# Eight shifted homes for the stationary tiles of the second feed-forward product

## The chip, the core and the metric

One core of a Trainium2 chip runs one program. The metric is the device time of one execution in microseconds (us), the median of several runs. The engines are named as in the profile: PE is the matrix unit (TensorE), PEld its loads of stationary operands, DVE is VectorE, ACT is ScalarE, POOL is GpSimd, SP is the engine whose queue starts the transfers.

## What is computed

The reference is one residual block of an encoder: 256 frames of width 2048 go through a norm, a retention branch and a latent-attention branch that gates merge, and then through a feed-forward part. The change lies in the feed-forward part, which is:

```python
z = _rmsnorm(h, norm_mlp_g[l]) @ w_up[l]            # 256 x 2048  times 2048 x 8192
h = h + jnp.square(jax.nn.relu(z)) @ w_down[l]      # 256 x 8192  times 8192 x 2048
return _rmsnorm(h, norm_f_g)
```

The second product, with `w_down`, is the last large piece of work in the program; the final norm follows it.

## The kernel before

**Products in three parts.** The kernel multiplies float32 numbers with the matrix unit's fp32r type. Each operand is split into a part `hi`, its value rounded to fp32r by a copy on ACT, and a part `lo`, the remainder that DVE computes by subtracting (`split`, lines 214 to 222, for activations; `weights`, lines 146 to 153, for weights). A product is then hi times hi, hi times lo and lo times hi, three matmuls into one accumulator.

**The first feed-forward product** (lines 792 to 800) takes 64 units of 128 hidden rows. A unit (`t_unit`, lines 170 to 175) loads two pieces of `w_up` of 512 KB, splits them, and runs 16 matmuls of 512 columns (line 159) and 16 of 256 columns (line 163). There the weights are the stationary operand, the activations `hT` the moving one. ACT and DVE join the two halves of the result, apply the squared ReLU and leave the unit in `hid` in SBUF (line 800). `hid` has 64 units in all, in four tiles, one of which (`hid3`) lies in the pool `hp`.

**The second product** (lines 818 to 832) runs over the same 64 units as its contraction. For unit `i`, line 822 splits `hid` into `dh` (ACT, line 216) and `dl` (DVE, line 217), each 128 partitions by 256 frames. Line 825 loads, casts and subtracts two halves of `w_down[i]`, each 128 by 1024. `down` (lines 807 to 816) then issues three matmuls for each of 2 frame blocks `t` and 4 column blocks `c`. In all three the stationary operand is a 128 by 128 block of `dh` (lines 814 and 815) or `dl` (line 816), and the moving operand is 512 columns of the weights' `hi` or `lo`. So a unit has 24 matmuls, each with a stationary load of its own, and the whole product has 1536. The results stay in eight PSUM accumulators `pd` over all 64 units. The last two units (`LAST`) are kept back and issued column block by column block, so that the accumulators end one after another and `finish` and `normalize` can begin.

**Where the tiles lie.** A tile is taken from a pool under a tag. Tiles of one tag share `bufs` homes (fixed addresses) in rotation, and a tile's first writer waits until the readers of the tile that had the home before are done. `dh` and `dl` have 3 homes each, of 256 float32, which is 1024 bytes in every partition. The weights' `hi` and `lo` have 4 homes each of 4096 bytes (line 143). In the program before, every home that the second product's matmuls read, stationary or moving, begins at byte 128 modulo 512 of its partition, and the blocks within it (128 frames, 512 columns) are whole multiples of 512 bytes. The same holds for nearly all other products of the kernel. One stage differs: the latent projection at `w_ckv` has weight tiles of 2 rows of 288 columns (1152 bytes), so that its moving operand begins at 128 for one row and at 256 modulo 512 for the other, while its stationary operand `x` is at 128.

**What sets the order.** A scheduler orders each engine's instructions by simulating the program; an engine then runs its own list in order. Matmuls of the last two units are held in the written order. All weight loads are issued from SP's queue into 5 homes `raw`.

Of the kernel before, what the change touches and what calls it, by code (L numbers as in the profile page):

```python
# [13 lines left out]
F32R = mybir.dt.float32r  # L14
# [5 lines left out]
P = 128  # L20
S = 256
# [10 lines left out]
QK_SCALE = float(192.0 ** -0.5)  # L32
LOWEST = -3.4e38
WARM = 8
MASKED = -3.0e38

MAGIC = 12582912.0
# [15 lines left out]
def _consts():  # L53
    c = np.zeros((P, N_CONST), np.float32)
    c[:, C_ID : C_ID + P] = np.eye(P)
    p = np.arange(P)
    own = np.where(p[None, :] // CHUNK <= p[:, None] // CHUNK, 0.0, MASKED)
    c[:, C_MASK : C_MASK + 128] = own
# [30 lines left out]
def block_kernel(ctx: ExitStack, tc: tile.TileContext, A):  # L89
# [46 lines left out]
    def atps(name):  # L136
        return pat.tile([P, 512], F32, tag="at", name=name)
# [8 lines left out]
    def weights(src, shape):  # L146
        raw, hi, lo = (wtile(kind, shape) for kind in ("raw", "hi", "lo"))
        load = nc.sync.dma_start(raw, src)
        if uid[0] < 40:
            tc.keep_in_program_order(load)  # L150
        SC.copy(hi, raw)  # L151
        V.tensor_tensor(out=lo, in0=raw, in1=hi.bitcast(F32), op=ALU.subtract)  # L152
        return hi, lo
# [60 lines left out]
    def split(hi, lo, val, scale=None):  # L214
        if scale is None:
            SC.copy(hi, val)  # L216
            V.tensor_tensor(out=lo, in0=val, in1=hi.bitcast(F32), op=ALU.subtract)
        else:
            SC.activation(hi, val, AF.Copy, scale=scale)
            V.scalar_tensor_tensor(  # L220
                lo, in0=val, scalar=scale, in1=hi.bitcast(F32), op0=ALU.mult, op1=ALU.subtract
            )
# [12 lines left out]
    spin = atps("spin")  # L235
    for _ in range(WARM):
        PE.matmul(spin, cold[:, :P], cold, start=True, stop=True)
# [529 lines left out]
    hp = ctx.enter_context(tc.tile_pool(name="hp", bufs=1))  # L767
# [39 lines left out]
    def down(i, t, c, w, hs):  # L807
        (hi, lo), (dh, dl) = w, hs
        ts = slice(t * P, (t + 1) * P)
        ws = slice(c % 2 * 512, c % 2 * 512 + 512)  # L810
        out = pd[t][c]
        end = i == FT - 1
        mm = tc.keep_in_program_order if i >= FT - LAST else (lambda ins: ins)
        mm(PE.matmul(out, dh[:, ts], hi[:, ws], start=i == 0, stop=False))  # L814
        mm(PE.matmul(out, dh[:, ts], lo[:, ws], start=False, stop=False))  # L815
        mm(PE.matmul(out, dl[:, ts], hi[:, ws], start=False, stop=end))  # L816

    tail = []
    for i in range(FT):
        dh = hp.tile([P, S], F32R, tag="dh", bufs=3, name=f"dh{i}")  # L820
        dl = hp.tile([P, S], F32R, tag="dl", bufs=3, name=f"dl{i}")
        split(dh, dl, hid[i // KT][:, i % KT])
        ws = []
        for half in range(2):
            w = weights(A["w_down"][i][:, half * 1024 : (half + 1) * 1024], [P, 1024])
            ws.append(w)
            if i < FT - LAST:
                for t in range(2):
                    for c in (2 * half, 2 * half + 1):
                        down(i, t, c, w, (dh, dl))  # L830
        if i >= FT - LAST:
            tail.append((i, ws, (dh, dl)))
# [113 lines left out]
```

## Time and profile before

| | |
|---|---|
| Median of 3 runs | 1631.72 us (1631.48 to 1631.87) |
| The profiled execution | 1632.22 us, of which its span is 1630.4 us |
| First product, by its chain of work | from about 925 to 1272.7 us of the span |
| Second product: first matmul to the start of the last | 1272.7 to 1620.6 us of the span |
| PE busy over the span | 1614.9 us (99%) |
| DVE busy, ACT busy | 996.2 us (61%), 809.7 us (50%) |
| Granted matrix clock over the span | 0.998 of full speed |
| HBM read | 300.84 MB, 186 GB/s over the span |

Times are from the span's start. The busy time of a matmul in the profile runs from its start to its modelled end, and overlaps that of the next one. How long a matmul holds the engine up is therefore read from the starts of two neighbours (the *step*), not from its own duration: in the second product a matmul lasts 389 ns, but the next begins well before that.

### The profile page before, as it was taken

To read this page: it belongs to the slowest core of one execution; us is meant where nothing else is said; L and a number is where in the kernel's file an instruction comes from. 1 tells how busy PE (TensorE), PEld (TensorE's weight loads), DVE (VectorE), ACT (ScalarE), POOL (GpSimd) and SP (SyncE) were. 2 spreads that over 40 slices of the span, in tenths; PEclk is the share of its full clock that TensorE was granted. 3 is DMA by queue.
4 is the path that set the end of the run, shared out by engine and by line. 5 is a ranking of instruction groups with operands and counts; after the bars stand their busy time and mean duration, and the time that the engine had idled before them with its cause. 6 is when DMAs were issued, how large, how long until landed. Compare 5 with 4: busy or idle time off the path is not lost.

```text
span 1630.4 us, 23041 instructions
## 1 busy us (share of the span) xinstructions
PE 1614.9 (99%) x8782; PEld 1398.8 (86%) x8782; DVE 996.2 (61%) x1491; ACT 809.7 (50%) x1249; POOL 49.5 (3%) x62
## 2 busy tenths in 40 slices
PE   8999999999999999999999999999999999999997
PEld 6888888888889889888888888888888888888886
DVE  7974588655556658666765555555555555555555
ACT  6544555544445556765545544444444444444444
POOL 7100000000000000000000000000000000000001
PEclk9999999999999999999999999999999999999999
DMA  8665544555556554325575555555555655555553
GB/s 306 200 233 193 187 156 166 169 192 186 190 170 203 190 191 146 125 94 176 186 246 187 174 193 188 192 189 186 191 192 184 223 194 192 193 193 195 192 194 112
DMA packets 84480, 304.46 MB, mean 187 GB/s; under 512 B 9360, under 2 KB 9488, under 8 KB 83600
## 3 DMA queue, kind: packets, MB, share of 16 engines
q1 hardware_dynamic: 84368, 302.98, 55.3%
q8 instruction: 69, 1.13, 0.3%
q14 instruction: 43, 0.35, 0.1%
HBM read 300.84 MB, written 2.10 MB: 186 GB/s over the span
## 4 chain that ended last, share of the span: by engine, by line
PE 97%; DVE 1%; issue 0%; DMA 0%; ACT 0%; POOL 0%; SPq 0%; DVEq 0%; POOLq 0%; ACTq 0%
PE z L159 14%; PE z L163 8%; PE dn L816 7%; PE dn L814 7%; PE dn L815 7%; PE rg L159 4%; PE yr L159 4%; PE gr L159 4%; PE gm L159 4%; PE mo L159 4%; PE qk L159 2%; PE gr L163 2%; PE yr L163 2%; PE gm L163 2%; PE rg L163 2%; PE mo L163 2%
## 5 line engine op out<-in xcount | busy, mean ns | idle before, releaser
L152 DVE TENSOR_TENSOR lo<-raw,hi 128x1024 fp32r<-128x1024 f32 (+2 forms) x562 | 666.0, 1204 | 521.6 <-ACT hi L151 248.3
L151 ACT CAST hi<-raw 128x1024 fp32r<-128x1024 f32 (+2 forms) x562 | 580.8, 1035 | 536.9 <-PE z L159 135.2
L159 PE MATMUL z<-hT,hi 128*128 128x512 f32 x1024 | 245.5, 391 | 0.0
L159 PEld LDWEIGHTS z<-hT,hi 128*128 128x128 f32 x1024 | 188.0, 188 | 36.1
L815 PE MATMUL dn<-lo,dh 128*128 128x512 f32 x512 | 199.2, 389 | 0.0
L816 PE MATMUL dn<-hi,dl 128*128 128x512 f32 x512 | 199.2, 389 | 0.0
L814 PE MATMUL dn<-hi,dh 128*128 128x512 f32 x512 | 198.9, 389 | 0.0
L163 PEld LDWEIGHTS z<-hT,lo 128*128 128x128 f32 x1024 | 131.6, 191 | 5.1
L163 PE MATMUL z<-hT,lo 128*128 128x256 f32 x1024 | 133.1, 283 | 0.0
L815 PEld LDWEIGHTS dn<-lo,dh 128*128 128x128 f32 x512 | 96.1, 188 | 20.1
L816 PEld LDWEIGHTS dn<-hi,dl 128*128 128x128 f32 x512 | 96.1, 188 | 19.9
L814 PEld LDWEIGHTS dn<-hi,dh 128*128 128x128 f32 x512 | 96.1, 188 | 19.8
L216 ACT CAST dh<-hid 128x256 fp32r<-128x256 f32 x64 | 26.0, 407 | 89.3 <-PE dn L815 89.3
L159 PE MATMUL mo<-my,hi 128*128 128x512 f32 x256 | 65.5, 396 | 0.4 <-DVE val L207 0.4
L159 PE MATMUL rg<-x,hi 128*128 128x512 f32 x256 | 64.0, 395 | 0.0
L159 PE MATMUL yr<-ry,hi 128*128 128x512 f32 x256 | 61.4, 391 | 0.0
L159 PE MATMUL gr<-x,hi 128*128 128x512 f32 x256 | 61.3, 391 | 0.0
L159 PE MATMUL gm<-x,hi 128*128 128x512 f32 x256 | 61.1, 391 | 0.0
L159 PEld LDWEIGHTS gm<-x,hi 128*128 128x128 f32 x256 | 47.0, 188 | 9.1
L159 PEld LDWEIGHTS gr<-x,hi 128*128 128x128 f32 x256 | 47.0, 188 | 9.0
L159 PEld LDWEIGHTS yr<-ry,hi 128*128 128x128 f32 x256 | 46.9, 188 | 9.0
L159 PEld LDWEIGHTS rg<-x,hi 128*128 128x128 f32 x256 | 46.2, 188 | 8.6
(271 smaller groups left out, 2239.1 us busy)
## 6 DMA issues: line engine op xcount, KB each, us to landing
raw<-w_up SPq DMA_DIRECT2D x128, 512.0 KB, 4.2
raw<-w_down SPq DMA_DIRECT2D x128, 512.0 KB, 4.3
raw<-w_rv SPq DMA_DIRECT2D x32, 512.0 KB, 4.5
raw<-w_rg SPq DMA_DIRECT2D x32, 512.0 KB, 4.5
raw<-w_gret SPq DMA_DIRECT2D x32, 512.0 KB, 4.3
raw<-w_ret_o SPq DMA_DIRECT2D x32, 512.0 KB, 4.6
raw<-w_gmla SPq DMA_DIRECT2D x32, 512.0 KB, 4.4
raw<-w_out SPq DMA_DIRECT2D x32, 512.0 KB, 3.7
```

The costliest lines, as they stand in the source:

```text
L151: SC.copy(hi, raw)
L152: V.tensor_tensor(out=lo, in0=raw, in1=hi.bitcast(F32), op=ALU.subtract)
L159: PE.matmul(out, w[0][:, k], x.both(k0 + k), start=start and k == 0, stop=False)
L163: PE.matmul(out[:, :S], w[1][:, k], x.hi(k0 + k), start=False, stop=stop and k == n - 1)
L216: SC.copy(hi, val)
L814: mm(PE.matmul(out, dh[:, ts], hi[:, ws], start=i == 0, stop=False))
L815: mm(PE.matmul(out, dh[:, ts], lo[:, ws], start=False, stop=False))
L816: mm(PE.matmul(out, dl[:, ts], hi[:, ws], start=False, stop=end))
```

## The change

The tiles `dh` and `dl` get eight tags each in place of one tag with 3 homes, chosen by the unit's number modulo 8, with one home for each tag. Each tile is allocated with 16 more float32 in every partition, of which none is used: only the first 256 columns are handed on. Nothing else is edited.

```diff
 WARM = 8
+SHIFT, SHIFTS = 16, 8
 MASKED = -3.0e38
...
     for i in range(FT):
-        dh = hp.tile([P, S], F32R, tag="dh", bufs=3, name=f"dh{i}")
-        dl = hp.tile([P, S], F32R, tag="dl", bufs=3, name=f"dl{i}")
+        dh, dl = (
+            hp.tile([P, S + SHIFT], F32R, tag=f"{kind}{i % SHIFTS}", name=f"{kind}{i}")[:, :S] for kind in ("dh", "dl")
+        )
         split(dh, dl, hid[i // KT][:, i % KT])
```

A home is now 1088 bytes, that is twice 512 and 64 more. The homes are taken in the order `dh0`, `dl0`, `dh1`, `dl1` and so on, so each begins 64 bytes further on, modulo 512, than the one before it. The eight homes of `dh` lie at four places modulo 512 that are 128 apart, each place twice, and those of `dl` at the four places between them; together they go through all eight multiples of 64. The two frame blocks of a tile, 512 bytes apart, have the same place. The moving operands stay where they were modulo 512. The homes of both kinds take 17,408 bytes of a partition in place of 6,144.

## The prediction

> **What bounds the kernel now.** I read the page's busy shares first, then the chain of waits, then the chain in order of time for the two feed-forward products, and last the instructions in order of time.
>
> ```profile
> span 1630.4 us, 23041 instructions
> PE 1614.9 (99%) x8782; PEld 1398.8 (86%) x8782; DVE 996.2 (61%) x1491; ACT 809.7 (50%) x1249; POOL 49.5 (3%) x62
> PEclk9999999999999999999999999999999999999999
> PE 97%; DVE 1%; issue 0%; DMA 0%; ACT 0%; POOL 0%; SPq 0%; DVEq 0%; POOLq 0%; ACTq 0%
> ```
>
> The first and second line give span and busy time, the third the granted clock in 40 slices, the fourth the chain's shares. PE is the chain, at full clock. Time can only come from fewer matmuls, which the change doesn't give, or from a shorter *step*, the time from one matmul's start to the next one's.
>
> The instructions that touch the product's accumulators `dn` (count, then minimum, median and maximum duration in ns, then first and last start):
>
> ```profile
> L814 PE MATMUL dn<-hi,dh x512: 389/389/396, 1272.7 to 1620.2; 128*128 128x512 f32 x171
> L816 PE MATMUL dn<-hi,dl x512: 388/389/389, 1273.1 to 1620.6; 128*128 128x512 f32 x171
> ```
>
> From the first L814 at 1272.7 to the last L816 at 1620.6 lie 347.9 us and 1535 steps: 226.6 ns each. This holds from end to end, so no wait on a transfer, on ACT or on DVE is left in the product. Its time is 1536 steps, and nothing else.
>
> What a step is made of, I read from the first product's matmuls of half the width, in the chain in order of time (start, duration, count):
>
> ```profile
> 1249.96 0.60 PE z L163 x5
> ```
>
> Five steps of 256 columns take 0.60 us, 120 ns each. The 256 columns that a 512-column matmul has more cost 226.6 - 120.0 = 106.6 ns, 0.4164 ns a column. So 512 columns stream in 213.2 ns and 256 in 106.6 ns, and 13.4 ns of each step are **excess** over streaming. Every one of these matmuls has a stationary load (188 ns long in the page's rows) beside it.
>
> **The change part by part.** *Removed and added instructions:* none. There are 64 casts to `dh`, 64 subtractions to `dl`, 1536 loads and 1536 matmuls before and after, and no transfer is added or moved: 0 us.
>
> *More homes, 8 in place of 3.* The split of a unit may run eight units ahead. Now it waits for its home:
>
> ```profile
> 1403.22 0.41 ACT L216 CAST dh<-hid 128x256 fp32r<-128x256 f32 x1 [1.44 <-PE dn L815]
> 1403.66 0.43 DVE L217 TENSOR_TENSOR dl<-hid,dh 128x256 fp32r<-128x256 f32 x1 [0.62 <-ACT dh L216]
> ```
>
> ACT waits 1.44 us for PE and then casts for 0.41 us; DVE follows with 0.43 us. With eight homes the cast waits for the same place in PE's order, once a unit, only for a later unit's tile; behind it on ACT stand the same casts of weights. Before the product begins, five more casts and subtractions (5 x 0.41 and 5 x 0.43 us) can move up into the first product. There a unit takes 5.56 us (16 steps in 3.65 us and 16 in 1.91 in the chain in order of time), and ACT works 0.37 + 1.05 + 1.05 = 2.47 us of it, DVE 2 x 1.18 + 0.42 + 0.42 = 3.20 us. The gaps of 3.1 and 2.4 us hide them, and the casts of weights that could queue behind them themselves wait for PE to release a home. I cost this at 0; without the cover it is 0.84 us, once or twice. The waits removed from ACT gain nothing, since PE waits for none of them. The cast's own speed at a shifted address can't matter either: 0.41 us in 5.44 us.
>
> *Other addresses.* This is all that can reach PE. Now each stationary block begins at the same place modulo 512 as the moving operand. After the change that holds for 2 of the 8 homes of `dh` and none of `dl`; with two of three loads from `dh`, 1/6 of the loads keep it and 5/6 lose it. The trace of before has one long stage where operands stand apart: the latent projection with rows of 288 columns, whose second row lies 128 bytes further modulo 512.
>
> ```profile
> 514.75 0.29 PE L199 MATMUL kv<-hi,x 128*128 128x288 f32 x1
> 514.88 0.29 PE L200 MATMUL kv<-hi,x 128*128 128x288 f32 x1
> 515.01 0.29 PE L199 MATMUL kv<-hi,x 128*128 128x288 f32 x1
> 515.14 0.30 PE L200 MATMUL kv<-hi,x 128*128 128x288 f32 x1
> 515.27 0.42 PE L202 MATMUL kv<-lo,x 128*128 128x288 f32 x2
> 515.53 0.29 PE L199 MATMUL kv<-hi,x 128*128 128x288 f32 x1
> ```
>
> These are starts and durations; the fifth row is two matmuls. Six steps take 515.53 - 514.75 = 0.78 us, 130.0 ns each. By the rule from 256 and 512 columns, 288 columns should take 288 x 0.4164 + 13.4 = 133.3 ns. So the only stage whose operands stand apart in half of its matmuls has 10.0 ns of excess, 3.3 ns less. I take that as the estimate for the new homes: 1536 x 3.3 = **5.1 us** less. If the whole effect belongs to the half that stands apart, it is 6.7 ns there, and in the second product 1536 x 5/6 x 6.7 = 8.6 us. I take the smaller value, because only one distance of eight is seen, and because width and address can't be told apart in that stage.
>
> The far ends. Below: all excess goes, 1536 x 13.4 = 20.6 us; I know no row that reaches it, and half of it, 10 us, is the practical end. Above: the step isn't fixed even now. The product's first matmuls, behind the narrow ones, start at
>
> ```profile
> 1272.66 0.40 PE L814 MATMUL dn<-hi,dh 128*128 128x512 f32 x1
> ...
> 1274.05 0.39 PE L814 MATMUL dn<-hi,dh 128*128 128x512 f32 x1
> ```
>
> six steps apart (two rounds of L814, L815, L816): 1.39 us, 232 ns each, 5 ns more than the settled step with the same tiles. If loads and streams out of step cost that always, 1536 x 5/6 x 5 = 6.4 us more; if in every matmul, 7.7 us.
>
> The Trainium skill's page "TensorE: Matmul & The Clock Gate" (Step-by-step, the step on LDWEIGHTS) says that the two operands have independent read ports and that loading the next stationary tile takes no read bandwidth from the running matmul. By that rule addresses don't matter and the sum is 0. The 0.78 us above doesn't contradict it outright, but nothing in it explains 10.0 ns where 13.4 were due.
>
> **The sum** is made against the profiled execution, 1632.22 us: a span of 1630.4 and 1.8 us around it. 0 + 0 - 5.1 gives 1627.1; that execution was 0.5 us above the median of 1631.72, so the forecast for the median is **1626.6 us**.
>
> **The rivals.** *No change.* The excess belongs to the handover from one stationary tile to the next and not to addresses. For it: a 256-column and a 512-column step have the same excess, and in the settled product neither ACT's nor DVE's traffic, at half of the time, disturbs the step. Against it: the 10.0 ns of the projection. Time 1631.7 us. That is also how the rule of the Trainium skill's page would come out.
>
> *Slower.* Equal places modulo 512 are the good case: load and stream run in a settled rhythm that the 226.6 ns are the mark of. With homes that move by 64 bytes the rhythm is broken, every unit runs as the first six steps do, and PE gives back 5 ns in 5/6 of the steps: 1631.7 + 6.4 = 1638.1 us. It decides as soon as the mean step is above 226.6 + 2.1 ns, which is 0.2%. For it: those 1.39 us. Against it: they end after a few steps and follow a change of width, and the projection, whose distance changes from row to row, shows no such loss.
>
> *The large gain.* Equal places are the worst of all, and all other distances lose at least half of the excess: 1536 x 5/6 x 6.7 = 8.6 us and up to 13 us, 1623 to 1618 us. For it: all other stages, with equal places, have the same 13.4 ns. Against it: the projection's rows at distance 128 would have to be the whole of its gain.
>
> *The change doesn't do what it says:* with a scheduler between, homes could come in another order. Then the places modulo 512 still differ, as the home is 1088 bytes; I give it nothing of its own.
>
> **How the numbers follow.** Forecast, a gain of 3.3 to 7 us: 0.38. Large gain: 0.10. No change: 0.27. Slower: 0.25. Faster by over 0.2% (3.3 us, about what a measurement of this kernel can tell from no change) is 0.48, within it 0.27, slower 0.25. The forecast's own range is 1624 to 1629 us. The range that holds 8 in 10 must take in the half of the excess below, 1617, and the slower case with every step disturbed, 1639.5: **1617 to 1640 us**.
>
> **What would show it.** Right: the `dn` matmuls' first and last start lie 342 to 344 us apart in place of 347.9, and the step differs from unit to unit in a cycle of four or eight units, since a home keeps its place. Starts in three successive units that differ by nothing would show the no-change case, and a uniform 5.44 us a unit with a changed time elsewhere would show that the order of the work moved. The product's stretch should be all of the difference: the first product, up to about 1272.7 us, should not move by more than 1 us. Wrong: units above 5.44 us, or any idle time of PE behind `dh` or `dl`, which would make the zero for the extra homes false.

## The result: 7 us slower, all of it in the second product's steps

The changed kernel takes 1638.7 us (1638.22 to 1639.03) against 1631.48 us (1631.10 to 1631.87) of the kernel before: a ratio of 1.0044, 95% interval 1.0029 to 1.0059. The forecast was 1626.6 us with a range of 1617 to 1640 us; the rival called *Slower* had given 1638.1 us.

The profile after, first lines of the page, then two rows of the instructions that touch `dn` (first and last start in us), then the chain in order of time at the end of the first product (start, duration, count). The line numbers are 1 higher than before.

```profile
span 1636.5 us, 23035 instructions
PE 1623.7 (99%) x8782; PEld 1399.6 (86%) x8782; DVE 996.2 (61%) x1491; ACT 809.2 (49%) x1249; POOL 49.8 (3%) x62
```

```profile
L815 PE MATMUL dn<-hi,dh x512: 387/389/404, 1271.7 to 1626.5; 128*128 128x512 f32 x171
...
L817 PE MATMUL dn<-hi,dl x512: 387/397/400, 1272.1 to 1627.0; 128*128 128x512 f32 x171
```

```profile
1266.25 3.65 PE z L160 x16
1269.90 1.91 PE z L164 x16
```

The counts of matmuls are the same, and the first product's units are what they were, 16 steps in 3.65 us and 16 in 1.91. The second product runs from 1271.7 to 1627.0 us: 355.3 us in place of 347.9, 7.4 us more in 1535 steps, 231.5 ns a step in place of 226.7. That it began 1 us earlier says nothing of the change: with the work ahead of it the same, it begins at 1271.5 us in the second experiment below and at 1272.7 us in the kernel before.

How the units lie within it is read from ACT's casts to `dh`, one a unit, each released by PE's last reading of an earlier unit's `dh`:

```profile
1404.98 0.41 ACT L217 CAST dh<-hid 128x256 fp32r<-128x256 f32 x1 [1.51 <-PE dn L816]
...
1410.51 0.41 ACT L217 CAST dh<-hid 128x256 fp32r<-128x256 f32 x1 [1.49 <-PE dn L816]
...
1416.09 0.41 ACT L217 CAST dh<-hid 128x256 fp32r<-128x256 f32 x1 [1.51 <-PE dn L816]
```

By these rows a unit takes 5.53 and 5.58 us in turns (5.54 and 5.58 us by the starts of the matmuls), in place of 5.44 us each time. The cycle has two units, not four or eight: a home of `dh` and the one two units later, 256 bytes further on, behave alike. ACT still waits for PE; the profile shows no idle time of PE within the product.

### The profile page after: what moved, and what is told of

The parts are those of the page before. It is cut to its first block, busy times and chain, and to the rows that moved or that the text cites. A ratio compares the mean times of both kernels' runs of the same rounds, so it can differ in the third digit from the quotient of the medians.

```text
span 1636.5 us, 23035 instructions
## 1 busy us (share of the span) xinstructions
PE 1623.7 (99%) x8782; PEld 1399.6 (86%) x8782; DVE 996.2 (61%) x1491; ACT 809.2 (49%) x1249; POOL 49.8 (3%) x62
## 4 chain that ended last, share of the span: by engine, by line
PE 97%; DVE 1%; ACT 0%; DMA 0%; issue 0%; POOL 0%; SPq 0%; DVEq 0%; POOLq 0%; ACTq 0%
PE z L160 14%; PE z L164 7%; PE dn L817 7%; PE dn L816 7%; PE dn L815 7%; PE rg L160 4%; PE yr L160 4%; PE gr L160 4%; PE gm L160 4%; PE mo L160 4%; PE qk L160 2%; PE gr L164 2%; PE yr L164 2%; PE gm L164 2%; PE rg L164 2%; PE mo L164 2%
## 5 line engine op out<-in xcount | busy, mean ns | idle before, releaser
L218 DVE TENSOR_TENSOR dl<-hid,dh 128x256 fp32r<-128x256 f32 x64 | 27.2, 425 | 44.8 <-ACT dh L217 44.8
```

## The experiments

All are edits of the kernel before, except the one that says otherwise. Where `dh` and `dl` are moved, they rotate through 3 homes as before, and the place of a tile is set by a slice of a wider home, the same for eight units in a row:

```diff
+        dh = hp.tile([P, S + 128], F32R, tag="dh", bufs=3, name=f"dh{i}")[:, at_h : at_h + S]
+        dl = hp.tile([P, S + 128], F32R, tag="dl", bufs=3, name=f"dl{i}")[:, at_l : at_l + S]
```

The second to the ninth experiment have one run each. What they show is read from blocks of units within one trace, and not from their times.

Below, the *distance* is the byte where the stationary block begins minus the byte where the moving operand begins, modulo 512.

**Eight homes without a shift.**

```diff
+            hp.tile([P, S], F32R, tag=f"{kind}{i % 8}", name=f"{kind}{i}") for kind in ("dh", "dl")
```

> Eight homes each for dh and dl, but of 1024 bytes, so that every home begins at 128 modulo 512 as before. If the number of homes and the order that the scheduler makes of them cost the 7 us, a unit of 24 matmuls takes 5.53 to 5.58 us as in the changed kernel and the time is about 1638.7 us. If the addresses modulo 512 alone cost it, a unit takes 5.44 us and the time is that of before, 1631.5 us.

Measured: 1631.15 us, ratio 0.9998 (0.9989 to 1.0008), every unit 5.44 us. The number of homes and the order of the work cost nothing. What is left is the addresses, or the padding as such; the eleventh experiment separates these two.

**`dh` and `dl` moved together.** `at_h = at_l = 16 * (i // 8)` float32.

> Three homes as before, and dh and dl both begin 64 * (i // 8) bytes further on modulo 512, so that eight units in a row keep one distance to the moving operand, and no step between dh and dl. Theory of the distance (what counts is how far the stationary block stands from the moving operand modulo 256 or 512): the blocks of units at 0 and 256 take 5.44 us a unit, those at the odd multiples of 64 and at 128 and 384 take 5.5 to 5.6 us. Theory of the jump (what counts is that one load's place differs from the load before it, as dh and dl do): every block takes 5.44 us, but for single steps where a block begins.

Measured: 1636.63 us. The casts at the borders of blocks of eight units (distance 64, 128, 192, 256):

```profile
1315.01 0.41 ACT L216 CAST dh<-hid 128x256 fp32r<-128x256 f32 x1 [1.44 <-PE dn L815]
...
1359.80 0.41 ACT L216 CAST dh<-hid 128x256 fp32r<-128x256 f32 x1 [1.52 <-PE dn L815]
...
1404.41 0.41 ACT L216 CAST dh<-hid 128x256 fp32r<-128x256 f32 x1 [1.50 <-PE dn L815]
...
1448.37 0.41 ACT L216 CAST dh<-hid 128x256 fp32r<-128x256 f32 x1 [1.47 <-PE dn L815]
...
1491.91 0.41 ACT L216 CAST dh<-hid 128x256 fp32r<-128x256 f32 x1 [1.44 <-PE dn L815]
```

Eight units take 44.79, 44.61, 43.96 and 43.54 us, which is 5.60, 5.58, 5.49 and 5.44 us a unit. The blocks at 320, 384 and 448 repeat those at 64, 128 and 192. So the distance counts, with a period of 256 bytes, and no jump between `dh` and `dl` is needed for the loss: the theory of the jump falls.

**`dl` alone.** `at_h = 0`, `at_l = 16 * (i // 8)`.

> Three homes as before; dh stays at the moving operand's place, dl begins 64 * (i // 8) bytes further on modulo 512. Theory of the jump: units whose dl stands apart take 5.5 us or more, with the most at 64 and 320, and those at 0 take 5.44 us. Theory of the distance: one of three loads stands apart, so a third of what the second experiment shows for the same distance, on the step during which dl is loaded. If distance modulo 256 is what counts, the unit at 256 takes 5.44 us under both.

Measured: 1637.04 us. Casts at the borders of the blocks with `dl` at 64 (the first two) and at 256:

```profile
1315.85 0.41 ACT L216 CAST dh<-hid 128x256 fp32r<-128x256 f32 x1 [1.44 <-PE dn L815]
...
1360.21 0.41 ACT L216 CAST dh<-hid 128x256 fp32r<-128x256 f32 x1 [1.49 <-PE dn L815]
...
1448.98 0.41 ACT L216 CAST dh<-hid 128x256 fp32r<-128x256 f32 x1 [1.49 <-PE dn L815]
...
1492.50 0.41 ACT L216 CAST dh<-hid 128x256 fp32r<-128x256 f32 x1 [1.45 <-PE dn L815]
```

44.36 and 43.52 us for eight units: 5.55 us a unit at 64, as at all the other distances, and 5.44 us at 256, as at 0. This is a miss for the theory of the distance in its simple form: with one load of three apart, a third of 0.16, 0.14 and 0.05 us was due, and 0.11 us came each time. A mixture of distances costs more than its share, so the price isn't a fixed sum for each load.

**All operands moved together.** The weights' `hi` and `lo` of `w_down` get wider homes as well, and the same `at`.

> dh, dl and the weights' hi and lo all begin 64 * (i // 8) bytes further on modulo 512, so that all stay at equal places while the place moves. If a place as such is dear (a home off a multiple of 128 or 256), blocks take 5.5 us and more as in the second experiment at the same shift. If only the distance between stationary and moving operand counts, or the jump between loads, every block takes 5.44 us and the time is about 1631.5 us.

Measured: 1631.74 us, 5.44 us a unit at every place, with some 0.04 us once at each border of blocks. So none of the eight places costs anything as such.

**The moving operand alone.** `dh` and `dl` stay, `hi` and `lo` begin `16 * (i // 8)` float32 further on.

> dh and dl stay where they are; the weights' hi and lo begin 64 * (i // 8) bytes further on modulo 512. Theory of the signed distance modulo 256 (stationary minus moving): the order of the second experiment's blocks is mirrored, 5.44 us a unit at shifts 0 and 256, 5.49 us at 64 and 320, 5.57 us at 128 and 384, 5.60 us at 192 and 448. If only the size of the distance or the stationary tile's own place counts: 5.60, 5.57 and 5.49 us at 64, 128 and 192, or 5.44 us everywhere.

Measured: 1637.40 us. Borders of the blocks with the moving operand 64, 128 and 192 bytes on:

```profile
1315.81 0.41 ACT L218 CAST dh<-hid 128x256 fp32r<-128x256 f32 x1 [1.44 <-PE dn L817]
...
1359.77 0.41 ACT L218 CAST dh<-hid 128x256 fp32r<-128x256 f32 x1 [1.47 <-PE dn L817]
...
1404.40 0.41 ACT L218 CAST dh<-hid 128x256 fp32r<-128x256 f32 x1 [1.51 <-PE dn L817]
...
1449.20 0.41 ACT L218 CAST dh<-hid 128x256 fp32r<-128x256 f32 x1 [1.52 <-PE dn L817]
```

43.96, 44.63 and 44.80 us for eight units, 5.49, 5.58 and 5.60 us: the order of the second experiment mirrored. What counts is the signed distance.

**The projection with 288 columns.** Its weight tiles get rows of 2048 bytes, so that both rows keep one place, which moves by 64 bytes with each fourth of the contraction.

```diff
+            wtile("raw", shape), *(wtile(kind, [P, 2, 512])[:, :, at : at + 288] for kind in ("hi", "lo"))
...
-                w = weights(A["w_ckv"][k // 2, half], [P, 2, 288])
+                w = weights(A["w_ckv"][k // 2, half], [P, 2, 288], 16 * (k // 4))
```

> The weight tiles of the latent projection with 288 columns get rows of 2048 bytes in place of 1152, so that both rows of a tile begin at the same place modulo 512; that place moves by 64 bytes with every fourth of the contraction (moving operand 0, 64, 128, 192 bytes on). If the shorter excess of that stage (10.0 ns a step) came from its rows that stand apart, as the prediction took it, the first fourth has steps of 133.3 ns and a later one fewer. If it came from the width of 288 columns, the first fourth has 130 ns or less, and by the distances of the second product the other fourths have more: about 2, 5 and 7 ns at distances of 192, 128 and 64.

Measured: 1632.59 us. Two pairs of starts six steps apart, the first with all operands at equal places, the second at distance 128:

```profile
495.77 0.29 PE L201 MATMUL kv<-hi,x 128*128 128x288 f32 x1
...
496.56 0.29 PE L201 MATMUL kw<-hi,x 128*128 128x288 f32 x1
...
511.73 0.29 PE L201 MATMUL kv<-hi,x 128*128 128x288 f32 x1
...
512.53 0.29 PE L201 MATMUL kv<-hi,x 128*128 128x288 f32 x1
```

0.79 and 0.80 us. Over the steady steps of a fourth, the steps are 131.7 ns at distances 0 and 192 and 133.3 ns at 128 and 64. Neither expectation is met in full. Equal places give 131.7, not 133.3, so half of the 3.3 ns was there without any distance: at this width the rule from 256 and 512 columns comes out too long. And a constant 128 gives 133.3, more than equal places, although the layout of before, with 0 and 128 in turns, has 130.0. The sequence is better than either of the distances that it is made of. (The rows' pitch went from 1152 to 2048 bytes with this edit; no run separates its part.)

**Finer distances.** `at_h = at_l` = 2, 4, 8, 12, 24, 40, 56 and 60 float32, that is 8 to 240 bytes.

> dh and dl both begin 8, 16, 32, 48, 96, 160, 224 and 240 bytes beyond the moving operand's place, eight units each. If places count in lines of 64 bytes, 8 to 48 bytes take 5.44 us a unit, 96 takes 5.60, 160 takes 5.57, 224 and 240 take 5.49 us. If the distance acts in finer steps, the units lie between their neighbours: 5.46 to 5.56 us from 8 to 48 bytes, 5.45 to 5.47 us at 224 and 240. If equal places are not the best but only the best of the multiples of 64, one of these is below 5.44 us.

Measured: 1640.49 us. Borders of the blocks with 96, 160, 224 and 240 bytes (of the last block, five units):

```profile
1451.00 0.41 ACT L216 CAST dh<-hid 128x256 fp32r<-128x256 f32 x1 [1.52 <-PE dn L815]
...
1495.98 0.41 ACT L216 CAST dh<-hid 128x256 fp32r<-128x256 f32 x1 [1.52 <-PE dn L815]
...
1540.78 0.41 ACT L216 CAST dh<-hid 128x256 fp32r<-128x256 f32 x1 [1.52 <-PE dn L815]
...
1585.58 0.41 ACT L216 CAST dh<-hid 128x256 fp32r<-128x256 f32 x1 [1.52 <-PE dn L815]
...
1612.78 0.41 ACT L216 CAST dh<-hid 128x256 fp32r<-128x256 f32 x1 [1.44 <-PE dn L815]
```

5.62, 5.60, 5.60 and 27.20 / 5 = 5.44 us a unit from casts five units apart. None of the three expectations holds. Together with the second experiment, for wide steps (a unit divided by 24):

| distance in bytes | 0 | 8 | 16 to 64 | 96 | 128 | 160 | 192 | 224 | 240 |
|---|---|---|---|---|---|---|---|---|---|
| unit, us | 5.44 | 5.54 | 5.60 | 5.62 | 5.57 to 5.58 | 5.60 | 5.49 | 5.60 | 5.44 |
| step, ns | 226.7 | 230.7 | 233.3 | 234.3 | 232.3 | 233.3 | 228.9 | 233.3 | 226.7 |

Equal places are the best that was found, 16 bytes before them are as good, 8 bytes behind them are already worse.

**The first product's weights.** There the weights are stationary; `hi` and `lo` of `w_up` begin `16 * (i // 8)` float32 further on.

> The stationary operand of the first feed-forward product, the weights' hi and lo, begins 64 * (i // 8) bytes further on modulo 512, units 2 to 63; hT stays. Theory of the distance: the 512-column steps (16 in 3.65 us before) become longer by 6.7, 5.6 and 2.3 ns at 64, 128 and 192, and nothing at 256, so that 16 take up to 3.75 us; the 256-column steps, whose load lasts about as long as the step, may lose more or less than these. If the effect belongs to the second product alone (its accumulators, or the same tile loaded twice), a unit keeps its 5.56 us at all shifts.

Measured: 1630.71 us. The chain in order of time, a unit at distance 64 and one at 256 (wide steps, then narrow ones):

```profile
987.58 3.73 PE z L162 x16
991.31 1.82 PE z L166 x16
...
1121.14 3.65 PE z L162 x16
1124.80 1.91 PE z L166 x16
```

The wide steps lose as in the second product: by the trace, once settled, 233.3, 232.6 and 229.1 ns at 64, 128 and 192. (At equal places too, the first five wide steps behind narrow ones take 228 to 236 ns; that is why 16 take 3.65 us and not 16 x 226.7 ns = 3.63 us.) The 256-column steps *gain*: 113.3, 118.6 and 115.6 ns in place of 120.0. At 64 a unit takes 5.55 us in place of 5.57, at 192 it takes 5.52 us on average, 5.49 and 5.54 in turns, and at 128 it takes 5.62, 5.61 and 5.64 us in a cycle of three. The weights' homes come round every two units, so a cycle of three can't be theirs: what the steps before leave behind sets the time of a unit too.

The loss of some distances and the gain of others nearly cancel over the product: the one run is at 1630.71 us, and the one of the kernel before beside it at 1631.16 us.

**Only the narrow steps' operand.** In the first product `lo` alone moves, by 16, 32, 48, 64, 96, 160, 224 and 240 bytes.

> In the first feed-forward product only lo, the stationary operand of the 256-column steps, begins 16, 32, 48, 64, 96, 160, 224 and 240 bytes beyond the moving operand's place, eight units each; hi stays at the moving operand's place. If the gain of the narrow steps at 64 bytes in the eighth experiment is theirs alone, units at 64 take 3.65 + 1.82 = 5.47 us in place of 5.56 us, and the 512-column steps keep 226.7 ns. If it was lent by the wide steps before them (load and stream left in another rhythm), the narrow steps take 120 ns again. The other distances show whether 113.3 ns is the floor; a step of 109 ns would be near the 106.6 ns of streaming.

Measured: 1630.90 us. At 64 the narrow steps take 117.8 ns and a unit 5.54 us; the shortest are 116.6 ns at 224 and 117.3 ns at 96 and 240 (5.53 us a unit), the longest about 120 ns at 160 (5.58 us). So of the 6.7 ns at 64, the narrow steps have only 2.2 ns when `lo` alone stands apart. The rest depends on the wide steps before them standing apart too: a step takes over a state that the last one left.

**A version that gains: `lo` 64 bytes on in the narrow steps with stationary weights.** Homes of `hi` and `lo` are 256 bytes longer, and a slice sets the place. The main lines of the edit; the kernel's other units of this form get the same places:

```diff
+        t = wp.tile([P, n + 64], dt, tag=kind, bufs=bufs, name=f"{kind}{uid[0]}")[:, at : at + n]
...
+        ws = [weights(src[:, half * HK : (half + 1) * HK], [P, HK, P], 0, 16) for half in range(2)]
...
+        hi, lo = weights(src, [P, 2, LT, P], 16, 16)
```

> All narrow matmuls with stationary weights get them 64 bytes beyond the moving operand's place: lo in every unit of 16 wide and 16 narrow matmuls (2560 narrow steps of the kernel), hi and lo in the low-rank pairs (480 steps); the wide ones and the second feed-forward product stay at distance 0. If the narrow steps' gain of 6.7 ns is their own, 3040 x 6.7 = 20 us at most, about 1612 to 1616 us. If it was lent by the wide steps, or given back where wide follows narrow, 1628 to 1632 us.

Measured: 1625.58 us, ratio 0.9964 (0.9951 to 0.9978). It lies between the two expectations: in the first product the narrow steps have 117.8 ns, and the wide ones settle at 226.7 as before.

**The changed kernel with steps of 256 bytes.** All eight rotating homes stay; only the padding differs.

```diff
-SHIFT, SHIFTS = 16, 8
+SHIFT, SHIFTS = 64, 8
```

> The changed kernel with its eight rotating homes, but 64 float32 of padding in place of 16: each home begins 256 bytes further on modulo 512 than the one before. Theory of the distance modulo 256: every unit takes 5.44 us and the time is that of before, 1631.2 to 1631.5 us. If the rotation of places as such costs, or the padding, or a place off 128 modulo 512, the time stays near 1638.7 us.

Measured: 1631.45 us, ratio 1.0000 (0.9991 to 1.0009), 5.44 us a unit. One number takes the whole loss back, and neither the padding nor the rotation costs anything as such.

**A better version: both parts 192 bytes on.** Again the main line of the edit, with the same for the kernel's other units of this form.

```diff
+        ws = [weights(src[:, half * HK : (half + 1) * HK], [P, HK, P], 48, 48) for half in range(2)]
```

> As in the tenth experiment for the low-rank pairs, but in the units of 16 wide and 16 narrow matmuls hi and lo both begin 192 bytes beyond the moving operand's place, where the eighth experiment had 5.516 us a unit in place of 5.566 us. If that holds for every such unit of the kernel (about 150), 150 x 0.05 = 7.5 us, with some 1 to 1.5 us of the low-rank pairs: 1622 to 1624 us. If the gain at 192 depends on what runs beside the first feed-forward product, the other units keep 5.566 us and the time is about 1627 us.

Measured: 1621.94 us, ratio 0.9942 (0.9929 to 0.9956), 9.8 us less than the 1631.76 us of the kernel before beside it, and just below the expected stretch. Two units of the first product, in the chain in order of time:

```profile
1199.98 1.88 PE z L171 x16
1201.86 3.68 PE z L167 x16
1205.54 1.81 PE z L171 x16
1207.35 3.66 PE z L167 x16
```

3.68 + 1.81 and 3.66 + 1.88 us are 5.49 and 5.54 us, in place of 5.57. The two kinds of unit alternate, although their places modulo 256 are the same; the narrow steps have 113.3 ns in one and 117.8 in the other. The wide steps pay some 0.02 us and the narrow ones gain 0.03 to 0.10 us.

## Why the prediction was wrong, step by step

**What bounds the kernel** was right: PE's steps and nothing else. The added time is 1535 steps that are 4.8 ns longer.

**Zero for the extra homes** was right. Eight unshifted homes have a ratio of 0.9998, and the changed kernel with steps of 256 bytes has 1.0000. Units above 5.44 us, which the prediction named as a sign against this zero, came from the addresses.

**What a step is made of** held for 512 and 256 columns: 226.7 and 120.0 ns are the marks of settled steps at equal places, with an excess of 13.4 ns that addresses can move. For 288 columns the rule came out 1.6 ns too long (133.3 against 131.7). In the runs the excess went from 6.7 ns (narrow, distance 64) to 21.1 ns (wide, distance 96).

**The failed step is the estimate from the projection**: "So the only stage whose operands stand apart in half of its matmuls has 10.0 ns of excess, 3.3 ns less. I take that as the estimate for the new homes: 1536 x 3.3 = 5.1 us less." The term had the wrong sign: it measured 7.4 us more, 4.8 ns a step. The sixth experiment shows what those 3.3 ns were. About half was there at equal places, which gave 131.7 ns and not 133.3. The other half belonged to the layout with two distances in turns: a constant distance of 64 or 128 gave 133.3 ns and one of 192 gave 131.7, so that standing apart as such made no step of this stage shorter. Besides, a distance acts differently by width: 64 bytes cost a step of 512 columns 6.7 ns and one of 288 columns 1.6 ns, and steps of 256 columns gain by it. Why the alternating layout helps at 288 columns, no run shows. A narrow stage was a wrong row for a wide one.

**The share of 5/6** was wrong in its count too. The period is 256 bytes and not 512, so 4 of the 8 homes of `dh` keep an equal place. But mixtures cost more than their share. In the changed kernel, units with `dh` at 0 or 256 and only `dl` apart lost 0.10 us, which is near the 0.11 us of the third experiment. Units with `dh` at 128 and `dl` at 192 bytes lost 0.14 us, as much as both at 128 did in the second experiment, where both at 192 lost 0.05 us.

**The rival *Slower*** had the right mechanism in outline and nearly the size: 5 ns in 5/6 of the steps, 6.4 us, with 1638.1 us as the time. Its first argument against, that the 232 ns of the product's first steps die out, was true of equal places. A distance keeps the steps there, at 228.9 to 234.3 ns. Its second argument against was the projection again. The first six steps of the product, which I put in the bounds, were the better row: same width, same tiles, same loads. That the time came within 0.6 us of 1638.7 is in part luck, since the share of 5/6 was wrong and the price of a step isn't one number: with the distance it goes from 0 to 7.6 ns. The rival *The large gain* took equal places for the worst of all; in steps of 512 columns no distance tried is better.

**The rule on two independent ports** (the Trainium skill, "TensorE: Matmul & The Clock Gate", the step on LDWEIGHTS) had been the no-change case. The runs disagree with what the prediction drew from it, that addresses don't matter: with the same matmuls at the same clock of 0.998, where the next stationary tile lies takes a wide step from 226.7 to as much as 234.3 ns. Moving the weights alone mirrors the order, with up to 6.7 ns, and moving all operands together costs nothing, so the two reads do act on each other here. Whether by bandwidth, no run shows.

**Open:** which of the two streams waits for which, and why the scale is 256 bytes with a good place 16 bytes before the equal one. The traces have starts and modelled ends, and no cause within a matmul.

## What to carry to other kernels

Where matmuls bound a kernel, read the step between starts against the width of the moving operand, and compare the first bytes of the stationary and the moving operand modulo 256. In this kernel's steps of 512 columns equal places were the best found, and nearly all other distances cost time, up to 3.4% of the step. Its steps of 256 columns with a load each were better off at 64 or 192 bytes. Measure such a thing with a few places in one kernel, a block of units for each: the cases then stand in one trace. And take a price from a row of the same width, even where it is a short one, before a row that only shares the feature in question.

## What the runs showed of the hardware that I had not expected

- The distance of the two operands acts modulo 256 bytes and with its sign: 64 bytes cost 6.7 ns a wide step, 192 bytes 2.3 ns; moving the other operand mirrors them.
- It is not smooth: 192 bytes have 228.9 ns, 160 and 224 bytes 233.3 ns, and 240 bytes 226.7 ns again.
- It has the opposite sign for steps of 256 columns: 113.3 ns at 64 bytes against 120.0 ns at equal places. Steps of 288 columns lie between: 133.3 ns at 64 and 128 bytes against 131.7.
- Steps hand something on. The same narrow steps at 64 bytes take 113.3 ns behind wide ones at 64 bytes and 117.8 ns behind wide ones at equal places.
